# Constant places for the moving operands of a one-core hybrid decoder layer: wider activation rows, shifted up tiles, a later weight pool and pinned splits

## The chip, the cores and the metric

The kernel runs on one core of one Trainium2 chip. The metric is the device time of one execution in microseconds. Names of engines in the profile: PE is TensorE's matmuls and PEld its weight loads, DVE is VectorE, ACT is ScalarE, POOL is GpSimd, SP is SyncE, which here issues nearly all DMAs.

## The reference

One layer on a residual stream of 1024 tokens with 16 meta tokens in front (L = 1040), width 1024, all in fp32:

```python
h = jnp.concatenate([meta, x], axis=1)
a = rmsnorm(h, ln_mix_pre)
proj = a @ w_in                                   # 1024 x 3584
dq, dk, dv, hq, hf, hi, hg = jnp.split(proj, SPLITS, axis=-1)
y_diff = diff_attention(dq, dk, dv, ...)          # 4 heads, two softmaxes each, o = (p1 - lam * p2) v
y_hgrn = hgrn2(hq, hf, hi, hg, ...)               # 4 heads, gated recurrence in chunks of 16
mix = jnp.concatenate([y_diff, y_hgrn], axis=-1) @ w_out
h = h + rmsnorm(mix, ln_mix_post)
a = rmsnorm(h, ln_ffn_pre)
u = causal_conv3(a @ w_ffn_up) + conv_b           # 1024 x 5632, width-3 convolution along the tokens
gate, up = jnp.split(u, 2, axis=-1)
y = (gelu(gate) * up) @ w_ffn_down                # 2816 x 1024
out = (h + rmsnorm(y, ln_ffn_post))[:, 16:, :]
```

## The kernel before, in words

Every fp32 product is made of three matmuls: each operand is split into a high part (a cast, `uh`, `woh`, `ahi`, mostly on ACT) and a low part (the difference, `ul`, `wol`, `alo`, on DVE or POOL), and PE adds high by high, high by low and low by high in one bank. A matmul has a stationary part of 128x128 (the weights' tiles) and a moving part of 256 to 512 columns.

The work goes through four stages.

1. *Norm, projections, attention, recurrence* (0 to 508 us). The normed tokens are transposed into `ahi` and `alo`, [128, 8, 1040]: one row of 4160 bytes for each k (k counts the 8 blocks of 128 along the width). The 28 projection tiles run over three groups of tokens (`GROUPS`: 272, 384 and 384 columns) in `proj_step` (L241-245) or, for the first tiles, in the class that holds L893. `interleave` feeds these matmuls into the holes of attention and recurrence, by a budget of time.
2. *Output projection* (508 to 633 us), in two halves of 512 columns. The mixed heads come back from DRAM as moving tiles `mp`; `load_wo` loads the output weights raw (`wor`, in the ring `wr`) and splits them into `woh` and `wol`; those of k = 0, 1 of the first half lie in the pool of the other weights, those of k = 2 to 4 in the pool `wosplit`, the rest in `wo`. The matmuls are L1020-1024 and, for the meta tokens, L1033. Behind the second half, `post(i)` adds the residual and norms token block i (`xh`, then `a`), `trans(i)` transposes it on PE (L1237) into `at`, and `t_split` splits sums of its quarters into the moving tiles `t{p}_{j}`.
3. *Up projection* (633 to 1063 us). The product of one 128-wide tile `ft` of gate and up is made as seven products of half size (a Strassen scheme, j = 0 to 6), for each half p of the tokens (`WN`: 258 and 256 columns). ft = 0 is made plainly (`plain_unit`, L1364-1366); for ft = 1 to 21, `unit` issues for each j and then each p twelve matmuls (L1383-1385), and the folds (`x1`, `u2`, `u3`, `ug`, `uu`) put the products together. `prep(q)`, q = 7 ft + j, makes the weights of one product: sums of raw quarters (`ws`) on POOL, the high part `uh` on ACT, the low part `ul` on DVE or POOL. `conv` and `gated` do convolution and gelu on DVE, ACT and POOL.
4. *Down projection* (1063 to 1285 us, L1546-1548), again by seven products, then norm and store.

A scheduler sets the order on each engine by priorities and by readiness in its own model; `tc.issue_after(mark)` puts what is issued inside it behind the marked instruction. A tile's place in the partition follows from the order in which pools are opened and the tiles' widths; `gap(pool, name, n)` spends n bytes of a partition to move what follows. Pools that are closed give their room to those opened later.

## Time and profile before

| | us |
|---|---|
| median of 3 runs (lowest to highest) | 1297.99 (1297.83 to 1299.12) |
| the profiled execution, its own time | 1296.03 |
| span of that execution | 1294.2 |
| PE busy | 1265.5 (98%) |
| DVE, ACT, POOL busy | 884.7, 694.4, 486.9 |

The granted TensorE clock was 0.998 in the profiled execution. Busy times of PE overlap from one matmul to the next, so a single matmul's duration in a row is longer than the time from its start to the next start; the starts tell the rate. A row of a wait or a timeline names the engine, the line, the output tile and the input tiles; helpers issue everything on DVE, ACT and POOL from one line (L53), so tiles tell them apart. What the profile's rows say is shown with the prediction.

### The profile page before, as it was taken

To read this page: it belongs to the slowest core of one execution; us is meant where nothing else is said; L and a number is where in the kernel's file an instruction comes from. 1 tells how busy PE (TensorE), PEld (TensorE's weight loads), DVE (VectorE), ACT (ScalarE), POOL (GpSimd) and SP (SyncE) were. 2 spreads that over 40 slices of the span, in tenths; PEclk is the share of its full clock that TensorE was granted. 3 is DMA by queue.
4 is the path that set the end of the run, shared out by engine and by line. 5 is a ranking of instruction groups with operands and counts; after the bars stand their busy time and mean duration, and the time that the engine had idled before them with its cause. 6 is when DMAs were issued, how large, how long until landed. Compare 5 with 4: busy or idle time off the path is not lost.

```text
span 1294.2 us, 26076 instructions
## 1 busy us (share of the span) xinstructions
PE 1265.5 (98%) x10154; PEld 1178.6 (91%) x10154; DVE 884.7 (68%) x1488; ACT 694.4 (54%) x1639; POOL 486.9 (38%) x387
## 2 busy tenths in 40 slices
PE   8999999999999999999989999999999999999996
PEld 7999999999989998778889999999999998888885
DVE  7564646464646574547897778778778786797686
ACT  8465466546654664346754544445445454464553
POOL 5231423141423310343076675676665730010121
PEclk9999999999999999999999999999999999999999
DMA  6344655183735532787412222222222247955363
GB/s 216 95 98 91 120 117 120 39 151 87 131 100 102 116 100 87 216 271 273 133 65 83 75 80 93 74 74 94 76 78 90 66 143 235 340 181 167 90 212 122
DMA packets 116418, 165.04 MB, mean 128 GB/s; under 512 B 10099, under 2 KB 57523, under 8 KB 116294
## 3 DMA queue, kind: packets, MB, share of 16 engines
q1 hardware_dynamic: 93062, 151.84, 36.4%
q0 software_dynamic: 23232, 11.54, 7.5%
q8 instruction: 80, 1.31, 0.4%
q14 instruction: 44, 0.36, 0.1%
HBM read 134.24 MB, written 52.17 MB: 144 GB/s over the span
## 4 chain that ended last, share of the span: by engine, by line
PE 47%; DVE 4%; ACT 2%; issue 1%; DMA 1%; DVEq 0%; SPq 0%; ACTq 0%
PE pd L1547 5%; PE pd L1548 5%; PE pd L1546 5%; PE pb L1383 4%; PE pb L1384 4%; PE pb L1385 4%; PE pa L1384 3%; PE pa L1383 3%; PE pc L1384 3%; PE pa L1385 3%; PE pc L1383 3%; PE pc L1385 3%; DVE c L53 1%; DVE xh L53 1%; DVE wl L53 1%
## 5 line engine op out<-in xcount | busy, mean ns | idle before, releaser
L1383 PE MATMUL pb<-t,uh 128*128 128x258 f32 x504 | 141.4, 281 | 3.8 <-DVE u L53 3.8
L1384 PE MATMUL pb<-t,uh 128*128 128x258 f32 x504 | 141.4, 280 | 0.0
L1385 PE MATMUL pb<-t,ul 128*128 128x258 f32 x504 | 140.9, 280 | 0.0
L1547 PE MATMUL pd<-wl,gh 128*128 128x512 f32 x308 | 120.4, 391 | 0.8 <-DVE wl L53 0.8
L1548 PE MATMUL pd<-wh,gl 128*128 128x512 f32 x308 | 120.1, 390 | 0.0
L1546 PE MATMUL pd<-wh,gh 128*128 128x512 f32 x308 | 120.0, 390 | 0.0
L53 DVE SCALAR_TENSOR_TENSOR c<-uu,cwt,c 128x514 f32<-128x514 f32 (+1 forms) x88 | 96.5, 1097 | 20.6 <-ACT c L53 19.9
L53 POOL TENSOR_TENSOR c<-c,c 128x514 f32<-128x514 f32 (+1 forms) x44 | 64.6, 1468 | 121.0 <-ACT c L53 118.3
L1383 PEld LDWEIGHTS pb<-t,uh 128*128 128x128 f32 x504 | 95.1, 189 | 4.2 <-DVE u L53 4.2
L1385 PEld LDWEIGHTS pb<-t,ul 128*128 128x128 f32 x504 | 95.3, 189 | 0.0
L1384 PEld LDWEIGHTS pb<-t,uh 128*128 128x128 f32 x504 | 95.1, 189 | 0.0
L1384 PE MATMUL pa<-t,uh 128*128 128x258 f32 (+1 forms) x336 | 94.8, 282 | 0.0
L1383 PE MATMUL pa<-t,uh 128*128 128x258 f32 (+1 forms) x336 | 94.6, 282 | 0.0
L1385 PE MATMUL pa<-t,ul 128*128 128x258 f32 (+1 forms) x336 | 94.4, 281 | 0.0
L1385 PE MATMUL pc<-t,ul 128*128 128x258 f32 (+1 forms) x336 | 94.2, 280 | 0.0
L1384 PE MATMUL pc<-t,uh 128*128 128x258 f32 (+1 forms) x336 | 94.2, 280 | 0.0
L1383 PE MATMUL pc<-t,uh 128*128 128x258 f32 (+1 forms) x336 | 94.0, 280 | 0.0
L53 DVE SCALAR_TENSOR_TENSOR c<-ug,cwt,c 128x514 f32<-128x514 f32 (+1 forms) x88 | 86.4, 982 | 1.0 <-ACT c L53 0.3
L53 ACT CAST uh<-ra 128x512 fp32r<-128x512 f32 x67 | 41.2, 616 | 61.2 <-PE pb L1384 39.1
L53 DVE TENSOR_TENSOR ul<-ra,uh 128x512 fp32r<-128x512 f32 x42 | 40.9, 973 | 47.7 <-ACT uh L53 45.2
L53 POOL TENSOR_TENSOR ul<-ws,uh 128x512 fp32r<-128x512 f32 x42 | 62.1, 1479 | 28.4 <-ACT uh L53 24.7
L1547 PEld LDWEIGHTS pd<-wl,gh 128*128 128x128 f32 x308 | 57.9, 188 | 14.0 <-DVE wl L53 2.1
(388 smaller groups left out, 4172.4 us busy)
## 6 DMA issues: line engine op xcount, KB each, us to landing
ra<-in_wup_dram SPq DMA_DIRECT2D x88, 256.0 KB, 2.9
mp<-msc SPq DMA_DIRECT2D x23, 512.0 KB, 5.1
tsc<-in_wdown_dram SPq DMA_DIRECT2D x44, 256.0 KB, 4.9
wi<-tsc SPq DMA_DIRECT2D x44, 256.0 KB, 2.8
gi<-gsc SPq DMA_DIRECT2D x33, 256.0 KB, 4.4
wi<-in_wdown_dram SPq DMA_DIRECT2D x33, 256.0 KB, 5.0
gsc<-c SPq DMA_DIRECT2D x22, 257.0 KB, 2.0
tsc<-in_wdown_dram POOLq DMA_DIRECT2D x22, 256.0 KB, 7.1
```

The lines of the kernel that those rows point to most:

```text
L53: ins = call(*args, **kw)
L1383: T.matmul(pt, hi[:, s], th[:, k], start=(first and k == 0), stop=False, skip_group_check=True)
L1384: T.matmul(pt, hi[:, s], tl[:, k], start=False, stop=False, skip_group_check=True)
L1385: T.matmul(pt, lo[:, s], th[:, k], start=False, stop=(k == 3), skip_group_check=True)
L1546: T.matmul(py, gh[:, s], wh, start=(k == 0 and pr not in (3, 7)), stop=False, skip_group_check=True)
L1547: T.matmul(py, gh[:, s], wl, start=False, stop=False, skip_group_check=True)
L1548: T.matmul(py, gl[:, s], wh, start=False, stop=(k == NH - 1), skip_group_check=True)
```

## The change

Six things are edited:

- `ahi` and `alo` get rows of 1152 elements (4608 bytes), `place(t)` puts 16 unused elements ahead of the second group of tokens, and a gap of 64 bytes stands ahead of both.
- Pads (`gap`, an offset in `t_tiles`) move the up projection's moving tiles of p = 0, so that all of them begin 64 bytes past the weights' rows modulo 256, and those of p = 1 stay 64 bytes ahead of it.
- The pool `wosplit` is opened after the activations' pool has been closed, and lies over it; a gap puts its rows at the common place of the other weights.
- The ring of raw weights `wr` has four buffers and not three; the squares at the end use it too.
- The split `t_7` of the first half is issued after block 7's root and scaling, by two marks.
- In ft = 1, the preparations for ft = 2 are put off: j = 0 behind the gelu's product on POOL, j = 3 to 5 behind the folds of the same step, j = 1 and 2 behind their step. `x1` and `u2` share one tile in the pool of the mix.

```diff
+WR = 4
+def place(t):
+    return t + (0 if t < start(3) else 16)
...
-    MIX = {"X0": 2064, "X1": 2176, "X2": 2064}
+    MIX = {"X0": 2064, "X1": 2176, "X2": 2080}
...
-    ws_cm, wsp = pool("wosplit", 6)
     at_cm, atp = pool("at", 1)
-    ahi, alo = (atp.tile([P, KD, L], F32R, tag=t, name=t) for t in ("ahi", "alo"))
+    gap(atp, "edge", 64)
+    ahi, alo = (atp.tile([P, KD, P * NBLK], F32R, tag=t, name=t) for t in ("ahi", "alo"))
...
-        T.matmul(pt, hi[:, s], ahi[:, k, t0:t1], start=(k == 0), stop=False)
+        ts = slice(place(t0), place(t0) + t1 - t0)
+        T.matmul(pt, hi[:, s], ahi[:, k, ts], start=(k == 0), stop=False)
...
     close(at_cm)
+    ws_cm, wsp = pool("wosplit", 6)
+    gap(wsp, "gap0", 384)
     wo_cm, wop = pool("wo", 7)
-    gap(wop, "gap0", 448)
...
-            raw = wp.tile([P, 512], F32, tag="wr", name=f"wor{n}_{k}", bufs=3)
+            raw = wp.tile([P, 512], F32, tag="wr", name=f"wor{n}_{k}", bufs=WR)
...
+    gap(ep, "gap5", 192)
     m7 = ep.tile([P, 8 * WN[0]], F32R, tag="e1", name="m7")...
+    gap(ep, "gap6", 128)
...
-        rstd_of(s2, s2, D)
-        V.scalar_tensor_tensor(a2[:r], xh[:r], s2, gfb[:r], ALU.mult, ALU.mult)
+        marks["scale"] = rstd_of(s2, s2, D)
+        marks["normed"] = V.scalar_tensor_tensor(a2[:r], xh[:r], s2, gfb[:r], ALU.mult, ALU.mult)
...
         for j, b in ((1, b22), (2, b11), (3, b12)):
+            if p == 0:
+                gap(where, f"gap4{j}", 128 if j == 1 else 192)
             t_split(p, j, b, where, f"t{p}_{j}")
...
         if i == 7:
-            t_split(0, 7, quarter(0, 7), mxp, "X2", MIX["X2"])
+            with tc.issue_after(marks["scale"].ins), tc.issue_after(marks["normed"].ins):
+                t_split(0, 7, quarter(0, 7), mxp, "X2", MIX["X2"])
         if i == 8:
-            t_split(0, 6, quarter(0, 6), mxp, "X1", MIX["X1"])
+            t_split(0, 6, quarter(0, 6), mxp, "X1", MIX["X1"], 16)
...
-    gap(tp, "gap1", 64)
+    gap(tp, "gap1", 128)
...
-        x1, u2, u3 = (xup.tile([P, WN[0]], F32, tag=t, name=f"{t}_{nm}")[:, :n] for t in ("x1", "u2", "u3"))
+        pair = mxp.tile([P, 768], F32, tag="ms", name=f"xu_{nm}", bufs=2)
+        x1, u2 = pair[:, :n], pair[:, WN[0]:WN[0] + n]
+        u3 = xup.tile([P, WN[0]], F32, tag="u3", name=f"u3_{nm}")[:, :n]
...
-            if j != 1:
+            if j != 1 and (ft > 1 or j > 3):
                 prep(7 * (ft + 1) + j)
             for u in units:
                 next(u)
-            if j == 1:
-                prep(7 * (ft + 1) + j)
             if (ft, j) == (1, 1):
                 with tc.issue_after(marks[1, 1].ins):
                     next(p1)
+                with tc.issue_after(marks["mult"].ins):
+                    prep(14)
+            elif ft == 1 and 2 < j < 6:
+                with tc.issue_after(marks["last"].ins):
+                    prep(12 + j)
+            elif j == 1:
+                prep(7 * (ft + 1) + j)
```

The order of PE's matmuls is the same in both kernels. On DVE, at the end of the second half of the output projection, this stood in the kernel before (`t_7` is the split, `xh_7464` and `a_7` are block 7's residual and norm, `t_6`, `tmp_7614` and `xh_7518` belong to block 8):

```order
738 L53 TENSOR_TENSOR t_7_7572<-at_0_6976,t_7_7572 128x1032
739 L53 SCALAR_TENSOR_TENSOR xh_7464<-y_6270,ssy,xh_7464 128x512
740 L53 SCALAR_TENSOR_TENSOR xh_7464<-tmp_7559,ssy,xh_7464 128x512
741 L53 TENSOR_TENSOR at_0_6976<-at_0_6976 128x4x258
742 L53 TENSOR_TENSOR tmp_7614<-py_8_7575,gpo 128x512
743 L53 SCALAR_TENSOR_TENSOR a_7_7558<-xh_7464,ssy,gfb 128x1024
744 L53 TENSOR_TENSOR t_6_7627<-at_0_6976,t_6_7627 128x1032
745 L53 SCALAR_TENSOR_TENSOR xh_7518<-y_6270,ssy,xh_7518 128x512
```

And in the changed kernel:

```order
737 L58 TENSOR_TENSOR at_0_6977<-at_0_6977 128x4x258
738 L58 SCALAR_TENSOR_TENSOR xh_7467<-y_6271,ssy,xh_7467 128x512
739 L58 SCALAR_TENSOR_TENSOR xh_7467<-tmp_7562,ssy,xh_7467 128x512
740 L58 SCALAR_TENSOR_TENSOR a_7_7561<-xh_7467,ssy,gfb 128x1024
741 L58 TENSOR_TENSOR t_7_7575<-at_0_6977,t_7_7575 128x1032
742 L58 TENSOR_TENSOR tmp_7617<-py_8_7578,msgpo 128x512
743 L58 TENSOR_TENSOR at_0_6977<-at_0_6977 128x4x258
744 L58 SCALAR_TENSOR_TENSOR xh_7521<-y_6271,ssy,xh_7521 128x512
```

`t_7` went from ahead of block 7's `xh` to behind its `a_7`, and `t_6` to somewhere behind block 8's `xh`.

On DVE, in the first steps of ft = 1, before (`c` are the convolution of ft = 0, `u` the folds of the two token halves, `ul` low halves of weights):

```order
766 L53 TENSOR_TENSOR ul_8002<-ra_11_7991,uh_8001 128x512
767 L53 TENSOR_TENSOR u_1_0_8008<-pb_0_8043,x_1_0_8007 128x258
768 L53 SCALAR_TENSOR_TENSOR c_0_0_7966<-ug_0_7642,cwt,c_0_0_7966 128x514
769 L53 SCALAR_TENSOR_TENSOR c_0_0_7971<-uu_0_7643,cwt,c_0_0_7971 128x514
770 L53 SCALAR_TENSOR_TENSOR c_0_0_7966<-ug_0_7642,cwt,c_0_0_7966 128x514
771 L53 SCALAR_TENSOR_TENSOR c_0_0_7971<-uu_0_7643,cwt,c_0_0_7971 128x514
772 L53 TENSOR_TENSOR u_1_1_8027<-pb_1_8057,x_1_1_8026 128x256
773 L53 TENSOR_TENSOR ul_8074<-ws_8071,uh_8073 128x512
774 L53 SCALAR_TENSOR_TENSOR c_0_1_8077<-ug_1_7819,cwt,c_0_1_8077 128x510
```

And in the changed kernel (`xu` is the tile that now holds `x1` and `u2`):

```order
767 L58 TENSOR_TENSOR ul_8083<-ra_11_8072,uh_8082 128x512
768 L58 SCALAR_TENSOR_TENSOR c_0_0_7972<-ug_0_7645,cwt,c_0_0_7972 128x514
769 L58 SCALAR_TENSOR_TENSOR c_0_0_7977<-uu_0_7646,cwt,c_0_0_7977 128x514
770 L58 SCALAR_TENSOR_TENSOR c_0_0_7972<-ug_0_7645,cwt,c_0_0_7972 128x514
771 L58 SCALAR_TENSOR_TENSOR c_0_0_7977<-uu_0_7646,cwt,c_0_0_7977 128x514
772 L58 TENSOR_TENSOR xu_0_7999<-pb_0_8033,xu_0_7999 128x258
773 L58 TENSOR_TENSOR xu_1_8017<-pb_1_8047,xu_1_8017 128x256
774 L58 SCALAR_TENSOR_TENSOR c_0_1_8061<-ug_1_7825,cwt,c_0_1_8061 128x510
```

The first fold stands behind the four convolution steps now, and no low half stands between the two groups of these steps.

On SP, ahead of the second half of the output projection, before (`wor_7` is its last raw weight, `ms`, `m` and `mp` are stores and loads of the mixed heads, `ra` raw up weights):

```order
158 L1132 DMA ra_11_7991<-in_wup_dram 128x512
159 L186 DMA msc<-ms_0_6838 128x2x128 x2
160 L1048 DMA mp_1_6929<-msc 128x2x512
161 L1048 DMA mp_1_6929<-msc 128x2x384
162 L1181 DMA m_7053<-msc 128x2x128
163 L186 DMA msc<-ms_1_6884 128x3x128 x2
164 L1181 DMA m_7053<-msc 128x2x128 x3
165 L186 DMA msc<-ms_2_6918 128x3x128 x2
166 L1181 DMA m_7053<-msc 128x2x128
167 L1183 DMA gpo<-in_gpost_dram 128x512
168 L995 DMA wor_7_7046<-in_wout_dram 128x512
```

And in the changed kernel:

```order
152 L1056 DMA mp_8_6869<-msc 128x2x384
153 L1003 DMA wor_7_7047<-in_wout_dram 128x512
154 L1206 DMA xh_7053<-in_meta_dram 2x1024
155 L1140 DMA ra_11_7811<-in_wup_dram 128x512
156 L1140 DMA ra_22_7813<-in_wup_dram 128x512
```

The load of `wor_7` went from behind the stores and loads of the mixed heads to ahead of them and of the raw up weights.

## The prediction

> **What bounds the kernel now.** I read the page first, then the waits of PE, then windows and the timeline of PE, and DVE's timeline where PE waited.

> ```profile
> span 1294.2 us, 26076 instructions
> PE 1265.5 (98%) x10154; PEld 1178.6 (91%) x10154; DVE 884.7 (68%) x1488; ACT 694.4 (54%) x1639; POOL 486.9 (38%) x387
> PEclk9999999999999999999999999999999999999999
> L53 ACT CAST uh<-ra 128x512 fp32r<-128x512 f32 x67 | 41.2, 616 | 61.2 <-PE pb L1384 39.1
> L53 DVE TENSOR_TENSOR ul<-ra,uh 128x512 fp32r<-128x512 f32 x42 | 40.9, 973 | 47.7 <-ACT uh L53 45.2
> ```

> PE is busy for 98% and never below the top tenth of its clock: the kernel is one stream of matmuls, and only two things can shorten it, the holes in that stream and the time from one matmul's start to the next. PE's waits (engine and line waited for, us in total, times, longest) give the holes near the change:

> ```profile
> PE pb L1383 <- DVE u L53: 3.8, 2, 2.5
> PE pa L1237 <- DVE a L53: 1.8, 2, 1.5
> PE py L1022 <- DVE wol L53: 0.9, 1, 0.9
> PE py L1020 <- ACT woh L53: 0.3, 1, 0.3
> ```

> The other thing shows in windows cut at the fourteen slots of one tile of the up projection (ft; each slot is twelve matmuls; j from 0 to 6, p=0 with 258 columns and p=1 with 256 in turn; x14 counts those cut at the edges):

> ```profile
> 836.60:838.05 1.45, 1.45 (x14) 1.00 0.39 143
> ...
> 840.86:842.27 1.42, 1.42 (x15) 1.00 0.10 12
> 842.27:843.69 1.42, 1.42 (x15) 1.00 0.53 173
> 843.69:845.05 1.36, 1.36 (x15) 1.00 0.52 194
> 845.05:846.48 1.43, 1.43 (x15) 1.00 0.00 0
> 846.48:847.84 1.36, 1.36 (x15) 1.00 0.50 192
> 847.84:849.27 1.43, 1.43 (x14) 1.00 0.04 11
> 849.27:850.69 1.42, 1.42 (x14) 1.00 0.00 0
> 850.69:852.11 1.42, 1.42 (x15) 1.00 0.00 0
> 852.11:853.47 1.36, 1.36 (x14) 1.00 0.00 0
> 853.47:854.94 1.47, 1.47 (x14) 1.00 0.77 236
> ...
> sum 19.71, PE 19.71; mean PE 1.41
> ```

> The same twelve 256-column matmuls take 1.36 us in j=2, 3 and 5 (113.3 ns each) and 1.42 in j=1 and 4 (118), with the clock at 1.00 in all, and with DMA at half load in two fast slots and none in a slow one. So neither the clock nor DMA makes it. What sorts the slots is the place of the tiles in the partition, worked out from the widths and gaps of the code. I write a moving tile's distance from the weights' rows modulo 256 bytes. All p=1 tiles are at -64; the p=0 tiles are at -128 (j=0), -64 (1 and 4), 0 (2, 5, 6) and +64 (3). Slots of the same place that follow slots of the same place have the same time (1 and 4; 2 and 5), and a p=0 tile at -64 leaves the p=1 slot behind it in the slow mode, the others in the fast. [...]

> **The change part by part.** The sum is made against the profiled execution, 1296.03 us (span 1294.2), which is 1.96 below the median of 1297.99. PE's program is the same, matmul for matmul; only places, and the order on the engines that feed it, move.

> *Up projection.* All seven p=0 tiles go to +64 and p=1 stays at -64, so every pair stands as j=3 does now. That pair takes 1.43+1.36 us; from unrounded starts, over all ft, 2.793. Seven are 19.55 against the sum of 19.71: 0.16 us in each of 21 ft (1 to 21), 3.4 us. [...] The plain products before them (L1364-1366) gain 0.1 at most, their p=1 tiles staying.

> *Projections (L241-245 and L893).* There are 28 tiles of 8x3 matmuls in each of three token groups: 672 of 272 columns and 1344 of 384. Rows of 4160 bytes move the distance by 64 with each k, so all four places are used in turn. First and last row of a run of 28 gaps of 384 columns, and of one of 7 gaps of 272:

> ```profile
> 503.12 0.33 PE L243 MATMUL pi_hg<-alo,wh_hg 128*128 128x384 f32 x1
> ...
> 508.00 0.34 PE L245 MATMUL pi_hg<-ahi,wl_hg 128*128 128x384 f32 x1
> ...
> 310.26 0.29 PE L243 MATMUL pi_hf<-alo,wh_hf 128*128 128x272 f32 x1
> ...
> 311.14 0.29 PE L245 MATMUL pi_hf<-ahi,wl_hf 128*128 128x272 f32 x1
> ```

> They give 4.88/28 = 174.3 ns and 0.88/7 = 125.7; over all the runs of the stage it is 174.75 and 125.84. With rows of 4608 bytes the first group stands always at -64, the others at +64. Sorted by place, today's gaps are 173.8 for 384 columns at +64 and 124.8 for 272 at -64: (174.75-173.8)x1344 = 1.3 us and (125.84-124.8)x672 = 0.7, in all 2.0. Today no place lasts longer than one k, so this is the least certain term. Its ends come from the output projection, whose k=2 to 4 weights lie at another distance than the rest; ten gaps of 512 columns each:

> ```profile
> 561.07 0.40 PE L1024 MATMUL py<-woh,mp 128*128 128x512 f32 x1
> ...
> 563.39 0.39 PE L1020 MATMUL py<-woh,mp 128*128 128x512 f32 x1
> ...
> 567.76 0.39 PE L1022 MATMUL py<-wol,mp 128*128 128x512 f32 x1
> ...
> 570.02 0.39 PE L1024 MATMUL py<-woh,mp 128*128 128x512 f32 x1
> ```

> At +64 a gap is 2.32/10 = 232 ns, at 0 it is 2.26/10 = 226. 226.7 per 512 columns is 170 for 384 and 120.4 for 272, at best a gain of 4.75x1344+5.4x672 = 10 us. 232 is 174 for 384, what they have now; the slow slots' share, 1.42/1.36 on top of the best, would make 177.5 and 125.7 and cost 2.75x1344 = 3.7. I take a gain of 1.6, near the sorted places, with ends of -4 and +10.

> *Output projection.* With `wosplit` now at the weights' common place, the k=2 to 4 matmuls (three of eight, about 144 of the 390) go from 230-232 to 226.7: 0.8 us at most, hardly below 0.4. I take 0.8.

> *Late output weights.* `wosplit` now lies over the activations, so nothing of k=2 to 4 can be split before the last projection matmul at 508.00. PE has the twelve matmuls of k=0 and 1 first, 12x0.23 = 2.7 us. The chain is one ACT cast (0.62) and one DVE difference (0.97), two more differences behind them at 0.97 each, while PE needs 6x0.23 = 1.38 us per k; ahead of them stand the last gate's small steps, and behind the waiting matmuls the rest of the stage. A wait of 0 to 1 us; I take 0.3.

> *Four raw buffers.* Between the halves of the output projection PE waited for the last weight, whose load stood on SP's queue behind the stores and loads of the norms:

> ```profile
> 571.18 0.39 PE L1033 MATMUL py<-wol,m 128*2 128x512 f32 x1
> 571.86 0.40 PE L1020 MATMUL py<-woh,m 128*2 128x512 f32 x1 [0.29 <-ACT woh L53]
> 573.19 0.40 PE L1022 MATMUL py<-wol,m 128*2 128x512 f32 x1 [0.93 <-DVE wol L53]
> ```

> These two starts are 0.68 and 1.33 us behind the one before them where 0.23 is usual: 1.55 us. With a fourth buffer the load is issued some fifteen rows earlier on SP and passes them. I take the whole 1.55.

> *Block 7's norm.* The t_7 split now follows block 7's Exp on ACT and its scaling on DVE:

> ```profile
> 626.60 1.23 DVE L53 TENSOR_TENSOR t<-at,t 128x1032 fp32r<-128x1032 f32 x1
> ...
> 631.71 1.28 DVE L53 SCALAR_TENSOR_TENSOR a<-xh,ssy,gfb 128x1024 f32<-128x1024 f32 x1
> ```

> Its 1.23 us and its ACT cast go from ahead of the scaling to behind it, and the wait of 1.5 us on L1237 goes with them. Block 8's xh isn't later for it: t_6 has left the place ahead of it. What waits for t_7 itself is the seventh plain product, behind the transposes. Gain 1.5.

> *The first ft.* The two waits of L1383 (holes of 1.4 and 2.4 us beyond a usual gap, 3.7 with what trails them) are for low halves that stand on DVE behind four convolution steps:

> ```profile
> 659.67 0.93 DVE L53 SCALAR_TENSOR_TENSOR c<-ug,cwt,c 128x514 f32<-128x514 f32 x1
> 660.53 1.79 DVE L53 SCALAR_TENSOR_TENSOR c<-uu,cwt,c 128x514 f32<-128x514 f32 x1
> ...
> 660.01 1.75 POOL L53 TENSOR_TENSOR ul<-ws,uh 128x512 fp32r<-128x512 f32 x1
> ...
> 640.00:680.00 40.00, 36.24 (x306) 35.83 (x305) 38.62 (x41) 26.12 (x42) 24.24 (x12) 1.00 0.16 54
> ```

> A step takes 0.93 us alone and 1.79 beside POOL's subtraction. Now the halves are made by POOL ahead of time, and the preparations of the next ft, with their sums on POOL, come later. But DVE is busy 38.62 us of these 40: the same convolution steps now stand ahead of the folds (u, uu) that free PE's banks, and about two steps' stretch, 1.5 us, should come back as a new wait there. Net gain 2.2, ends 0 and 3.7.

> The renamed small tiles and the squares' ring stand clear of what follows them by over a microsecond; I put them at nothing, or 0.5 us if a ring turns.

> Sum: 3.4+0.1+1.6+0.8-0.3+1.55+1.5+2.2 = 10.9 us. 1296.03-10.9 = 1285.1 for the like of the profiled run, 1297.99-10.9 = **1287.1** for the median.

> **The rivals.** *Places are worth nothing.* Then only holes close: 1.55+1.5+2.2-0.3 = 5.0, so 1293.0. [...] The trace disagrees in the result: something at equal clock takes 0.06 us in one slot and not in the other. 0.10.

> *The holes move, and do not close.* DVE at 38.62 of 40 us is the bound in the first ft, and each early hole turns up at the next fold or transpose; only the streams gain, 3.4+0.1+1.6+0.8-0.3 = 5.6: 1292.4. For it, the saturated window; against, that two of the three places are simple orders of one instruction. 0.12.

> *Constant places lock the dear phase (slower).* Today's changing places mix dear and cheap; one place throughout can stay in the dear. The plain p=1 products do, first and last of 96:

> ```profile
> 643.42 0.36 PE L1364 MATMUL pq<-t,uh 128*128 128x256 f32 x1
> ...
> 654.69 0.28 PE L1366 MATMUL pq<-t,ul 128*128 128x256 f32 x1
> ```

> 11.27/95 = 118.6 ns and not 113.3, at -64 all through. If all up pairs entered that mode, seven p=1 slots at 1.42 and p=0 at 1.43 make 19.95 us, 0.24x21 = 5.0 lost in place of 3.5 gained; the projections lose 3.7 in place of 1.6. It decides where these losses, 8.7 in all, exceed the holes' 5.0 and the outputs' 0.8; then 1297.99+8.7-5.8 = 1300.9. Against it, j=3 enters the fast mode today from just such a pair. 0.10.

> *Projections lock the cheap phase.* Gain 10 in place of 1.6: 1278.7; half of it 1283. [...] 0.08.

> **How the numbers follow.** The forecast keeps 0.60. Its own range is 1284 to 1290.5, from the ends of the projections (half), the first ft and the late weights. The range of 1281 to 1294 adds both cases of partial gain and half of the cheap lock; out of it are the slower rival and most of the cheap one. About 0.2%, 2.6 us, is what a measurement here can tell: faster takes all but the slower rival and the worst of the partial cases, 0.85; same 0.06; slower 0.09.

> **What would show it.** Right: fourteen slots of 19.55 us with each p=1 slot at 1.36; runs of L241-245 at 174 ns or below; all runs of L1020-1024 at 226; no wait of L1020, L1022 at the second half, none over 0.5 of L1237, and a wait of at most 2 us for a fold in the first ft, where L1383's 3.8 stood. Wrong: p=1 slots at 1.42 or runs at 178 (the dear lock), slots as before (places do nothing), or waits of 5 us in all at new lines (the holes moved).

## The result, and the profile after

The change made no difference: 1298.97 us median of 14 runs (1297.43 to 1303.49) beside 1298.68 for the kernel before in the same rounds (14 runs, 1297.05 to 1300.76). The ratio is 1.0006, 95% interval 0.9996 to 1.0015. The forecast was 1287.1, range 1281 to 1294, and the time lies above it. The profiled execution of the changed kernel took 1298.48, that of before 1296.03.

The page of the kernel after, and PE's waits in it:

```profile
span 1296.7 us, 26036 instructions
...
PE 1261.1 (97%) x10154; PEld 1174.8 (91%) x10154; DVE 885.1 (68%) x1488; ACT 693.2 (53%) x1639; POOL 485.4 (37%) x387
...
PEclk9999999999999999999998999999999999999998
```

```profile
PE pb L1398 <- DVE xu L58: 8.2, 2, 6.8
...
PE py L1030 <- POOL wol L58: 2.2, 1, 2.2
...
PE pq L1378 <- DVE t L58: 1.8, 1, 1.8
...
PE pl L473 <- DVE am L58: 1.1, 1, 1.1
...
PE py L1028 <- ACT woh L58: 0.5, 1, 0.5
```

PE is busy for 4.4 us less and the span is 2.5 us longer. The waits that the prediction named are gone from their lines (L1383 is L1398 now), and others have come, one of them 6.8 us long. One slice inside PE's clock row is an 8 now (680 to 713 us); the 8 at its end lies behind the last matmul.

The streams did what was forecast. Slots of the up projection (j=0 to 2, and the sum of all fourteen, the windows being cut as before):

```profile
840.53:841.97 1.43, 1.43 (x14) 1.00 0.00 0
841.97:843.32 1.36, 1.36 (x14) 1.00 0.00 0
843.32:844.76 1.44, 1.44 (x14) 1.00 0.00 0
844.76:846.12 1.36, 1.36 (x14) 1.00 0.00 0
846.12:847.55 1.43, 1.43 (x14) 1.00 0.33 104
847.55:848.91 1.36, 1.36 (x14) 1.00 0.45 171
...
sum 19.55, PE 19.55; mean PE 1.40
```

19.55 is the forecast to the hundredth, and every p=1 slot is in the fast mode, at 1.36 us. The last run of a projection, and the first matmul of the output projection (508.18 in the trace before):

```profile
499.65 0.34 PE L249 MATMUL pi_hg<-alo,wh_hg 128*128 128x384 f32 x1
...
504.51 0.34 PE L251 MATMUL pi_hg<-ahi,wl_hg 128*128 128x384 f32 x1
504.68 0.39 PE L1028 MATMUL py<-woh,mp 128*128 128x512 f32 x1
```

28 gaps in 4.86 us are 173.6 ns; over the stage, 173.5 where 174.7 stood, and 123.7 where it was 125.8 for 272 columns. The stage ends 3.5 us earlier, twice the forecast of 1.6.

Since the order on PE is the same, each matmul's start can be set against its own start before. Where the difference changes tells where the time went:

| stretch | term of the sum | forecast, us | measured, us |
|---|---|---|---|
| to 508 | projections | -1.6 | -3.5 |
| 508 to 518 | late output weights | +0.3 | +2.0 |
| 518 to 629, streams | output projection | -0.8 | -0.9 |
| 566 to 576 | four raw buffers | -1.55 | +0.9 |
| 631 to 634 | t_7 behind the norm | -1.5 | -1.8 |
| 634 to 655 | (plain products) | -0.1 | +1.6 |
| 655 to 680 | first ft, net | -2.2 | -2.9 |
| 683 to 696 | ft = 2 | 0 | +9.7 |
| 700 to 1070 | up projection | -3.4 | -3.0 |
| to the end | down projection | 0 | +0.5 |
| sum | | -10.9 | +2.6 |

One row holds most of the miss, 9.7 of 13.5 us. PE at ft = 2, and its clock in windows from the hole on (columns: PE busy, granted clock, DMA share, GB/s):

```profile
682.54 0.28 PE L1400 MATMUL pc<-t,ul 128*128 128x256 f32 x1
689.64 0.58 PE L1398 MATMUL pb<-t,uh 128*128 128x258 f32 x1 [6.83 <-DVE xu L58]
```

```profile
689.64:692.00 2.36, 2.35 (x11) 0.50 0.39 115
692.00:694.00 2.00, 2.00 (x11) 0.50 0.35 131
694.00:696.00 2.00, 2.00 (x13) 0.61 0.00 0
696.00:698.00 2.00, 2.00 (x19) 1.00 0.06 9
```

A hole of 7.1 us from start to start, and then 5.9 us at half the clock, in which 2.8 more are lost: 9.7 in all with the usual gap taken off. What PE waited for is the fold `xu` (u2 of ft = 2, p = 0), which frees the bank that product j=3 adds to. The rows of DVE, ACT and POOL that stand ahead of it:

```profile
667.75 1.30 POOL L58 TENSOR_TENSOR c<-c,c 128x510 f32<-128x510 f32 x1 [2.02 <-ACT c L58]
669.00 1.29 POOL L58 TENSOR_TENSOR ws<-ra,ra 128x512 f32<-128x512 f32 x1
670.37 1.29 POOL L58 TENSOR_TENSOR ws<-ws,ra 128x512 f32<-128x512 f32 x1
...
671.69 0.62 ACT L58 CAST uh<-ws 128x512 fp32r<-128x512 f32 x1 [4.08 <-POOL ws L58]
...
672.34 1.12 DVE L58 TENSOR_TENSOR ul<-ws,uh 128x512 fp32r<-128x512 f32 x1 [3.15 <-ACT uh L58]
...
682.16 1.76 DVE L58 SCALAR_TENSOR_TENSOR c<-ug,cwt,c 128x514 f32<-128x514 f32 x1
...
689.18 0.41 DVE L58 TENSOR_TENSOR xu<-pb,xu 128x258 f32<-128x258 f32 x1
```

The mark holds the sums (`ws`) behind gelu's product on POOL at 667.75; two sums and a cast later, at 672.34, the next low half can start on DVE, which has stood still for 3.15 us by then. The fold comes at 689.18, behind ft = 1's convolution, some of whose steps take 1.76 us where others take 0.74. In the kernel before, the same fold starts at 686.47 and PE doesn't wait for it. So the hole has two parts: PE is there 4.6 us earlier, and the fold comes 2.7 us later.

### The profile page after: what moved, and what is told of

Read it like the earlier page. It is cut to its first block, busy times and chain, and to the rows that moved or that the text cites. A ratio compares the mean times of both kernels' runs of the same rounds, so it can differ in the third digit from the quotient of the medians.

```text
span 1296.7 us, 26036 instructions
## 1 busy us (share of the span) xinstructions
PE 1261.1 (97%) x10154; PEld 1174.8 (91%) x10154; DVE 885.1 (68%) x1488; ACT 693.2 (53%) x1639; POOL 485.4 (37%) x387
## 4 chain that ended last, share of the span: by engine, by line
PE 44%; DVE 6%; ACT 2%; issue 1%; DMA 1%; POOL 0%; DVEq 0%; SPq 0%; ACTq 0%; POOLq 0%
PE pd L1567 5%; PE pd L1568 5%; PE pd L1566 5%; PE pb L1398 4%; PE pb L1399 4%; PE pb L1400 4%; PE pa L1399 3%; PE pc L1399 3%; PE pa L1398 3%; PE pc L1398 3%; PE pa L1400 3%; PE pc L1400 3%; DVE c L58 1%; DVE t L58 1%; DVE xh L58 1%
## 5 line engine op out<-in xcount | busy, mean ns | idle before, releaser
L1398 PE MATMUL pb<-t,uh 128*128 128x258 f32 x504 | 142.0, 282 | 8.2 <-DVE xu L58 8.2
L1398 PEld LDWEIGHTS pb<-t,uh 128*128 128x128 f32 x504 | 96.1, 191 | 8.6 <-DVE xu L58 8.6
L1398 PE MATMUL pa<-t,uh 128*128 128x258 f32 (+1 forms) x336 | 93.9, 279 | 0.0
L1398 PE MATMUL pc<-t,uh 128*128 128x258 f32 (+1 forms) x336 | 93.7, 279 | 0.0
```

The source lines that it names most:

```text
L1398: T.matmul(pt, hi[:, s], th[:, k], start=(first and k == 0), stop=False, skip_group_check=True)
```

## The experiments

**The preparations.** By the code, the put-off preparations are those of products 0 to 3 of ft = 2: product 0 behind the gelu's product on POOL (the mark `mult`), products 1 to 3 behind the folds of steps 3 to 5 of ft = 1; products 4 to 6 keep their place. The first pair of runs undoes the new order in the changed kernel, and puts it alone into the kernel before.

```diff
-            if j != 1 and (ft > 1 or j > 3):
+            if j != 1:
                 prep(7 * (ft + 1) + j)
...
+            if j == 1:
+                prep(7 * (ft + 1) + j)
...
-                with tc.issue_after(marks["mult"].ins):
-                    prep(14)
-            elif ft == 1 and 2 < j < 6:
-                with tc.issue_after(marks["last"].ins):
-                    prep(12 + j)
-            elif j == 1:
-                prep(7 * (ft + 1) + j)
```

> The changed kernel with the order of preparations in ft = 1 of the kernel before; nothing else undone. Theory A (the put-off preparations leave DVE idle for 3.2 us and crowd it later, which makes the hole of 7.1 us at ft = 2 and the half clock behind it): both go, 9.8 us with the 2.8 of the half clock, and the first ft's own waits come back, 2.5. 1299.0-9.8+2.5 = 1291.7. Rival B (PE is only early at a DVE that is full anyway, the order of preparations is indifferent): a hole of 4 to 5 us stays between ft = 1 and ft = 2, with the half clock, 1297 to 1299.

> The kernel before with only the new order of preparations in ft = 1. Theory A: the two waits of L1383 in ft = 1 go (-2.5) and a hole of 5 to 7 us with half clock (2.8) comes at ft = 2: 1303 to 1306. Rival B: waits move at equal sum, 1298 to 1300. Rival C (the hole comes from the earlier arrival through the gains ahead of it): the hole is under 3 us, clock whole, 1297 to 1299.

With the old order 1297.9 (ratio 0.9994, 0.9984 to 1.0004), 6 us above what theory A said; the trace of this kernel is read further down, from its repeat. With the new order alone 1302.9 (1.0032, 1.0020 to 1.0044), at the lower end of what A said: 4 us slower than before, with the same hole where the kernel's other edits are absent:

```profile
690.38 0.58 PE L1383 MATMUL pb<-t,uh 128*128 128x258 f32 x1 [6.71 <-DVE u L53]
```

So the new order makes the hole by itself. Which part of it does, the next run tells: the changed kernel with the `mult` mark alone taken out.

```diff
-                with tc.issue_after(marks["mult"].ins):
-                    prep(14)
+                prep(14)
```

> The changed kernel with one mark taken out: the first preparation for ft = 2 no longer waits for the gelu's product on POOL, so its sums on POOL come ahead of the convolution; those of j = 3 to 5 stay behind the folds. Theory A: DVE's idle time of 3.2 us ahead of this preparation's low half goes, the hole at ft = 2 shrinks from 7.1 to 4 or less, and if that is too short for the clock to fall, its 2.8 go too: 1293. Rival B: the hole stays at 6 to 7, 1298 to 1299.

1296.8 (0.9984, 0.9974 to 0.9994). In its trace the wait at ft = 2 is 2.5 us and the clock behind it whole; DVE has no idle time ahead of the low half.

```profile
690.82 0.39 PE L1398 MATMUL pb<-t,uh 128*128 128x258 f32 x1 [2.53 <-DVE xu L58]
```

DVE's busy time in windows (columns as above, with DVE's busy time first): one row of the changed kernel, then the whole stretch here.

```profile
670.00:680.00 10.00, 6.77 (x8) 1.00 0.42 129
```

```profile
640.00:650.00 10.00, 10.00 (x10) 1.00 0.03 10
650.00:660.00 10.00, 10.00 (x10) 0.83 0.01 2
660.00:670.00 10.00, 9.71 (x11) 1.00 0.22 79
670.00:680.00 10.00, 8.98 (x13) 1.00 0.32 105
680.00:690.00 10.00, 10.00 (x13) 1.00 0.09 32
```

Of 50 us DVE is busy 48.7. So the mark makes most of the hole. What is left of it, 2.7 us by the starts, is about as much as the first ft gained (2.9). I read this as a full DVE that hands the hole on to the next fold; the other put-off preparations, which stay put off here, are not ruled out by this run. The second of the five rows also shows half clock, in this run behind another hole, of 2.06 us at 650. The time was forecast at 1293. Beside the changed kernel's, this profile gains 7.0 us from 683 to 700, but loses 1.6 at 566 to 576 and 1.6 at 645 to 655, each with half clock behind the same hole as there, and 1.9 at 576 to 592, where a new hole stands.

Does the backlog begin with ft = 0's convolution? Here its two DVE taps are left out.

```diff
-        V.scalar_tensor_tensor(c, u[:, 1:1 + w], cwt[:, m, 1:2], c, ALU.mult, ALU.add)
-        V.scalar_tensor_tensor(c, u[:, 0:w], cwt[:, m, 0:1], c, ALU.mult, ALU.add)
+        if ft:
+            V.scalar_tensor_tensor(c, u[:, 1:1 + w], cwt[:, m, 1:2], c, ALU.mult, ALU.add)
+            V.scalar_tensor_tensor(c, u[:, 0:w], cwt[:, m, 0:1], c, ALU.mult, ALU.add)
```

> The changed kernel whole, but the eight convolution steps of ft = 0 on DVE are left out (its first two taps are not added). Theory A (the hole of 7.1 us at ft = 2 is DVE's backlog, begun by these steps and by the 3.2 us in which DVE then waits for the put-off preparations): hole and half clock go, 9.8 us, and the wait of 1.7 in the first ft too: 1287.5 to 1289.5. Rival B (the preparations themselves come too late): a hole of 3 to 7 us stays near ft = 2, 1293 or more.

1295.2 (0.9967, 0.9955 to 0.9980), not 1288. PE's wait, and the row of DVE ahead of it:

```profile
687.57 0.58 PE L1399 MATMUL pb<-t,uh 128*128 128x258 f32 x1 [5.30 <-DVE xu L58]
```

```profile
669.89 1.11 DVE L58 TENSOR_TENSOR ul<-ws,uh 128x512 fp32r<-128x512 f32 x1 [3.39 <-ACT uh L58]
```

Theory A in the form "a backlog from ft = 0" falls. With eight steps less the hole is still 5.6 us, and DVE still idles for 3.39 on the put-off sums: what comes too late is the preparation, as rival B says.

**The places alone.** The changed kernel with the old preparations, `t_7` without marks and three raw buffers. The late output weights, the shared tile of `x1` and `u2` and the squares in the raw ring stay in it.

> The changed kernel with all its reorderings undone: old order of preparations, t_7 without marks, three raw buffers. What stays is the places and the late output weights. By the trace of the changed kernel the streams give 3.4 (projections), 3.1 to 3.3 (up) and some 0.5 (output projection), and the late output weights cost 2, or more with three raw buffers than with four (3): 1298.7-7+2.5 = 1294.2. If the streams' gains were lost again at the next wait of a full DVE: 1297 to 1299.

> The run with the places alone once more. If the places are what brings the gain and the three reorderings together bring nothing: 1293 to 1296, 3 us or more below the kernel before. If the first result was a good draw: 1297 to 1298.

1294.0 (0.9967, 0.9956 to 0.9978) and, repeated on another chip, 1294.75 (0.9966, 0.9954 to 0.9978). This is the best of all the kernels that compute the whole, some 4.4 us faster than before, and the forecast of 1294.2 from the pieces held. The three reorderings together take all of it back (1.0006 for the changed kernel).

**What each reordering does.** From the places alone: with the marks of `t_7`; with the fourth buffer (both differ from it by those lines of the diff alone); and both, the run with old preparations again.

> The run with the places alone (1294.0) plus the two marks of t_7; still the old order of preparations and three raw buffers. Theory A (the first ft and the fourth raw buffer are what costs; the marks of t_7 give their 1.7 us): 1292.3. Rival B (the marks of t_7 are what made the run with the old preparations slow, since the plain products then wait for t): 1296 to 1298.

> The run with the places alone (1294.0) plus the fourth raw buffer; old order of preparations, t_7 without marks. Theory A (with four buffers the low half of one weight of the second half stands on POOL behind two sums and another low half, and PE waits 2.6 us for it at 567 us; against it the wait of 1.6 for the last weight is gone, and the late weights wait 1 less): 1294 to 1297, with the hole at 567 in the trace. Rival B: 1292 to 1293, no hole there.

> The run with the old order of preparations once more. Theory A (a full DVE between 630 and 690 us sets the time of that stretch; the hole at ft = 2 goes, and holes of 2.6 and 1.2 to 2.8 us in the first ft stand in its place, one of them with half clock behind it in part of the runs): 1296 to 1298, a trace with holes near 663 and 672 us and none over 1 us at ft = 2. Rival B (the first result was a bad draw): 1291 to 1293, no hole over 1.7 us in the first ft.

1297.1 (0.9988, 0.9975 to 1.0001), 1297.7 (0.9991, 0.9979 to 1.0002) and 1298.9 (0.9996, 0.9985 to 1.0008). Each ratio is 2 to 3 thousandths above that of the places alone. For both steps together this is clear of noise (0.9996 beside 0.9966 on the same chip); for one alone, measured on another chip than the places, it is hardly so. The traces tell more. With the marks the wait at 633 us is gone from the trace (1.7 us gained), and 16 us later a plain product waits for its moving tile; with four buffers PE waits in the second half of the output projection. One row of each:

```profile
649.63 0.39 PE L1378 MATMUL pq<-t,uh 128*128 128x256 f32 x1 [1.83 <-DVE t L58]
```

```profile
570.11 0.50 PE L1030 MATMUL py<-wol,mp 128*128 128x512 f32 x1 [2.17 <-POOL wol L58]
```

The order of POOL tells the second: with three buffers `wol_4` of the second half follows `wol_6` directly; with four, two sums and a low half for the up projection stand between, since their raw data come earlier. That costs 2.3 us and the wait saved at the half's last weight is 1.1 to 1.5. In the last of the three runs ft = 2 costs nothing more than before (-0.2 us from 683 to 700), which confirms that the new order made the hole there. But holes of 1.1 and 3.1 us stand in the first ft, as theory A said, and three stretches of half clock: one behind the hole at 570, and two behind holes of 2.08 and 3.08 us:

```profile
652.00:655.00 3.00, 3.00 (x16) 0.50 0.02 5
...
676.50:680.00 3.50, 3.50 (x16) 0.50 0.34 97
```

The run with the first preparation early and three buffers joins the two findings.

> The changed kernel with the first preparation for ft = 2 early (as in the run with that alone, 1296.8) and three raw buffers. By the traces the hole of 2.6 us at 567 and the one at 591 go and the wait of 1.6 for the last output weight comes back; the first ft and ft = 2 together cost what they cost in the kernel before: 1294 to 1295. Rival (POOL's early sums hold up others wherever they go): 1296.5 or more.

1296.6 (0.9974, 0.9963 to 0.9986). Faster than before, not better than the places alone. The hole at 567 us is gone, and half clock shows twice in its profiled execution, whose time of 1300.3 is the longest of the eight.

**Is it DVE's load?** Three runs, all with the old preparations and three raw buffers. The first splits the output weights of k = 2, 3 early again. The second also gives two splits of the second token half's moving tiles to POOL, which is idle there. The third is the first without the marks of `t_7`. The diff is that of the second:

```diff
+    ws_cm, wsp = pool("wosplit", 4)
+    gap(wsp, "gap0", 384)
     at_cm, atp = pool("at", 1)
-    gap(atp, "edge", 64)
-    ahi, alo = (atp.tile([P, KD, P * NBLK], F32R, tag=t, name=t) for t in ("ahi", "alo"))
+    gap(atp, "edge", 192)
+    ahi, alo = (atp.tile([P, KD, 1088], F32R, tag=t, name=t) for t in ("ahi", "alo"))
...
-    ws_cm, wsp = pool("wosplit", 6)
-    gap(wsp, "gap0", 384)
...
-            elif k < 5 if n == 0 else k > 5:
+            elif k < 4 if n == 0 else k > 5:
...
-        V.tensor_tensor(lo, src, hi.bitcast(F32), op=ALU.subtract)
+        (G if (p, j) in ((1, 0), (1, 4)) else V).tensor_tensor(lo, src, hi.bitcast(F32), op=ALU.subtract)
```

> The run with places and the marks of t_7 (old order of preparations, three raw buffers), with the output weights of k = 2 and 3 split early again: rows of 4352 bytes (also 0 modulo 256) leave room for a pool of four ahead of the activations; k = 4 goes to the other pool. Places as before it. Theory A (the late pool held the raw buffers, so the loads of the last weights were issued after the last projection matmul and PE waited 2 us for them at 512 to 516 us): these waits go, 2 us or a little more with three raw buffers, and the projections keep their 3.5 us with the narrower rows: 1297.1-2.3 = 1294.8. Rival B (the loads are late for another reason): no change at that place.

> As the run with early output weights, and two of the splits of the second token half (t1_0 and t1_4) make their low half on POOL, which is idle there, and not on DVE. Theory A (from 633 to 690 us the time is DVE's, which is full, and every hole closed there opens again at the next fold): 2.4 us of DVE's work less, so the waits between 645 and 675 us lose 1 to 2.5 us. Rival B (the order is what matters, not the load; or POOL slows DVE's two-input steps by as much): no gain, or a loss of up to 2.

> As the run with early output weights, without the marks of t_7. By the traces the marks gain 1.7 at 631 us and lose 1.9 at 647: if a full DVE only moves the hole, the same time within 0.7 us. If the marks gain: 1.5 more than the run with them. If they cost (the timed runs with the places alone were 3 us below those with the marks): 1.5 to 3 less.

With early weights the waits at 512 to 516 us are gone from the trace (0.2 us where 2.0 were added), so the late pool was their cause; in the changed kernel six loads of output weights are issued only between 506.6 and 516 us, behind the last projection matmul. But the time is 1297.3 (0.9984, 0.9973 to 0.9995), no better than without: 2.5 us come back at 570, where low halves on POOL are late, and holes of 1.4 to 1.9 us appear in attention that I can't explain. The tiles on POOL cost 3 us more, 1300.4 (1.0007, 0.9996 to 1.0018): PE waits for POOL's split and then longer for DVE's.

```profile
646.96 0.39 PE L1378 MATMUL pq<-t,uh 128*128 128x256 f32 x1 [1.23 <-POOL t L58]
653.75 0.39 PE L1378 MATMUL pq<-t,uh 128*128 128x256 f32 x1 [2.28 <-DVE t L58]
```

Rival B holds, with a loss of 3 where it said up to 2: the two splits take 2.9 us each on POOL, where DVE takes 1.2, and a sum on DVE beside them takes 3.4 us and not 1.2. Without the marks 1298.1 (0.9990, 0.9979 to 1.0001), 0.75 from the run with them, which is within the noise: here the marks only move the hole.

**The squares' ring, and another place for the projections.**

```diff
-        sq = wp.tile([P, 512], F32, tag="wr", name=f"sq{m}_{c}", bufs=WR)
+        sq = fp.tile([P, 512], F32, tag="sq", name=f"sq{m}_{c}")
```

> The run with places and marks of t_7, and the squares of the last stage in a tile of their own again instead of the raw ring. Theory (the ring puts one low half of the weights behind two sums on DVE at the start of the fifth down product, a hole of 0.6 to 1.5 us at about 1142): 1 us less than without, 1291 to 1292. Rival: the order stays and so does the time.

1295.4 (0.9978, 0.9965 to 0.9991). DVE's order at the fifth down product is the old one again, but a low half is still waited for 12 matmuls later, 1.16 us, so the ring wasn't the cause; what is stays open.

```diff
-    return t + (0 if t < start(3) else 16)
+    return t + (0 if t < start(3) else 48)
...
-    gap(atp, "edge", 64)
+    gap(atp, "edge", 128)
```

> As the one with the squares' own tile, and the activations moved by 64 and 48 columns so that all three groups of the projections stand at distance 0 from the weights, where the down and the output projections keep 226.7 ns per 512 columns. If the distance sets the mode whatever the width, the gaps fall to 170 and 120.4 ns, from 173.4 and 123.7: (3.4x1344+3.3x672) = 6.8 us less, 1285. Rival (a narrower matmul leaves the weight load less room, and place 0 is no better than the others): 0 to 3 more.

The activations are moved by 64 bytes and the second and third group of tokens by 48 columns in place of 16. 1298.0 (0.9994, 0.9982 to 1.0005): 2.6 us slower than the run before it, which has the places of the change. The first matmul behind the projections shows where:

```profile
507.81 0.39 PE L1028 MATMUL py<-woh,mp 128*128 128x512 f32 x1
```

That is 3.1 us later than the 504.68 of the kernel after, and 3.3 later than the 504.51 of the run that differs in the place alone. The mean gaps are about 175 and 125.5 ns, near those of the kernel before, where the places took turns. So the place alone, with nothing else moved, is worth 3 us here, and 0, where the 512-column matmuls of the kernel before keep 226.7 ns beside 232 at 64, is the worse of the two for the 384 and 272 columns here. My rule from the one width didn't carry over.

## Why the prediction was wrong

**Streams: right.** The up term was right by its own step (a pair at 2.79, 19.55 in each ft); that such pairs keep their time one behind the other was assumed, and the run shows it. The projections were mis-sized on the safe side, 3.5 for 1.6: one constant place settles lower (173.5 and 123.7 ns) than the same place did between others (173.8 and 124.8). The rival "places are worth nothing" is refuted by the run at place 0: 173.5 or about 175 ns by the place alone. Through what the place acts, no run here shows; only that it acts.

**Late output weights: the chain was read, its head was not.** The step took one cast and one difference per k from 508 us on. It left out that raw buffers not yet split hold back the loads of the last weights; 2.0 us for 0.3.

**Four raw buffers: wrong in sign.** The load was indeed earlier. I followed it on SP and not on POOL, where earlier raw data of the up weights moved sums ahead of a low half that PE waits for.

**Block 7's norm: right at its place, wrong in the sum.** 1.8 us gone there, 1.6 back 16 us later. The prediction looked for the next wait at `t_7` itself. The tile that PE waits for is a split of the second token half (256 columns): DVE ends it at 647.6 us in the changed kernel and at 647.5 in the kernel before, so PE comes earlier and DVE doesn't. That queue was priced at nothing.

**The first ft: right at its place, and the step that failed the whole.** The net gain of 2.2 was 2.9. "What is late next" was looked for in the same ft, with 1.5 us. The working quoted DVE at 38.62 of 40 us and still booked 3.7 us of closed holes in and just ahead of this stretch (1.5 and 2.2). With DVE full, PE's earlier arrival at the next fold is itself a wait; and the mark put 3.15 us of idle time into DVE's fullest stretch. The fold one ft later was never costed: 9.7 us for 0. Nor was the clock: the profile showed it at full in all rows and I took that for given.

The rival nearest to the result is "the holes move, and do not close" (0.12). The profiles bear it out. From 625 to 700 us, counted between the same two matmuls in every run, PE is idle for 5.3 us in the kernel before. Where the first preparation waits for the mark `mult` it is 7.1 to 10.0 us, with two splits on POOL 8.9, and in the eleven other profiles, whatever the order, 4.3 to 6.8; the forecast needed 1.6. The rival had the mechanism and a price of 0 for it; the runs show that the move had a price of its own. The slower rival, the dear lock, did not come about.

**The base.** The profiled execution of before is 2.65 us below the median of its 14 runs; its trace has no half clock ahead of the last matmul. So of the 2.6 us in the table the timed runs show only 0.3. That flattered nothing in the terms, but it hid what a hole can cost in other executions.

## What to carry to other kernels

Where an engine that feeds TensorE is busy for 96% of a stretch (here DVE, for 38.62 of 40 us), an order that removes a wait there should be booked at nothing until the next thing due on that engine has been found, one stage further on, and its time worked out. A mark that puts work off is priced by the longest chain behind it (here POOL sum, cast, low half), and by what stands in order behind that chain's last step. Places of operands within 256 bytes are worth trying one at a time, with nothing else changed: here they brought 4.4 us that three well-meant reorderings hid.

## What the runs showed of the hardware

```profile
569.49 0.50 PE L1030 MATMUL py<-wol,mp 128*128 128x512 f32 x1 [2.16 <-POOL wol L58]
```

```profile
560.00:570.00 10.00, 7.90 (x35) 1.00 0.68 189
570.00:580.00 10.00, 9.94 (x36) 0.83 0.97 354
580.00:590.00 10.00, 10.00 (x46) 1.00 0.38 138
```

At half clock a step of 3.41 us costs up to half its length, by estimate 1.7 us; behind the hole at ft = 2, 5.9 us at half clock lost 2.8. A hole of 7 us takes far more than 1.95 us out of some step wherever it falls, so the half clock there is not luck: it stands behind the waits of 6.83, 6.71 and 5.30 us, in the changed kernel, with the new order alone and without ft = 0's taps.

It fits what the steps cost that the runs of most kernels spread over 4 to 10 us (1291.7 to 1298.1 for the places alone) and that in most of them the mean clock is lower where the time is longer, but no run here varied that alone, so it is argued and not shown.

Of the two places measured, the projections' better one differs from that of wider matmuls: 173.5 ns at 64 bytes, about 175 at 0 for 384 columns, while 512 columns take 232 at 64 and keep 226.7 at 0. Why is open.
